# Hybrid decoder layer: memory values by seven products in half of their k groups, and the order of work at three places

## The chip, the core and the metric

The kernel runs on one core of one Trainium2 chip. The metric is the time of one execution in microseconds: median 1534.65 of three runs, 1532.35 to 1535.73. Engines: PE is TensorE, DVE is VectorE, ACT is ScalarE, POOL is GpSimd, SP is SyncE, which issues most DMAs.

## The reference

One layer in float32 with 256 positions and 256 memory tokens, width 2048. What matters here:

```python
x = x + hybrid_mixer(rms_norm(x, mix_g), w_in, ...)       # causal pooling | gated delta rule, 8 heads
mem_h = rms_norm(mem, mem_norm_g)
kv = mem_h @ w_xkv                                         # keys: columns 0..2047, values: 2048..4095
pr = softmax(q @ k.T / sqrt(512)); x = x + (pr @ v) @ w_xo # 4 heads of 512
gate = causal_dwconv(h @ w_gate, conv_w, conv_b)           # h = rms_norm(x, ffn_g), 5632 columns
x = x + (silu(gate) * (h @ w_up)) @ w_down
return rms_norm(x, final_norm_g)
```

`kv` is one of seven large products; its value half is 256 x 2048 by 2048 x 2048. The decay of the delta rule comes from two small columns per head, which are scaled by the row norm of x, so it waits for the sum of squares of x.

## The kernel before

**Products.** Each float32 product is made of three TensorE products. An operand is rounded by ACT into a high part (L101, "cast") and VectorE subtracts that from the operand for the low part (L102, "remainder"); high by high, high by low and low by high go into the same PSUM bank. Weights pass one way: SP loads a raw tile of 1 MB (three buffers, tag `raw`), ACT casts and VectorE subtracts in pieces of 128 x 1024 (four buffers each, tags `whi`, `wlo`), TensorE multiplies.

**Stages**, one after the other on TensorE: input projection (eight key heads, then queries, values and gates, then pooling groups); memory keys (16 column tiles); memory values; the mixer's output; cross attention's queries; attention; its output `xo` (16 tiles, each followed by two residual additions on VectorE, L706 and L707); gate and up; down. Side work stands in lanes: generators whose next step `pump` issues behind a given matmul.

**Values.** Four column tiles of 512 by four k groups of 512: `pvs` has two PSUM banks, one for each half of the positions, and each of the 16 loads is split in two pieces and multiplied by both halves (L680 to L695): 4 x 16 x 2 x 3 = 384 matmuls of 512 columns.

**Gate and up.** Eleven blocks `b`, each of 1024 weight columns. Two of four k groups (`JS`) go by Strassen's scheme in Winograd's form: the 2 x 2 pieces of the operands are added and subtracted so that seven products do for eight; the other two (`JP`) go plainly. A block is a list of 22 steps (`KINDS` by group); "11", "22", "s3", "s1", "s2", "21", "s4" are the seven products, "p0" to "p3" the plain pieces. A step of the first kind is six matmuls (L882 to L884), a plain one twelve. `load` issues the weight tile of a step, `prepare` makes cast and remainder four steps ahead, and GpSimd adds a second tile by an accumulating DMA (L993) where the sum of two is wanted. `combine` and `finish_block` join the six banks `b1`, `b2`, `b3`, `b5`, `b6`, `b7` into rows c11, c12, c21, c22, which are transposed (L922) in the next block. The tiles "11" lie in `ring`, whose memory was the attention output's `oT`; all other weight tiles in a pool of eight (tag `wr`). The stationary operand is `hP`, made by `stationary(f)` in the residual's lanes, and sums of it.

**Beside the first gate block** the residual x itself is transposed and written out (`rows_of_x`, lane "xr": per step four transposes, one copy on ACT into a tile of tag `sg` with two buffers, one write by SP). The last row's norm `r3` is computed there too (`last_row`).

**Start.** x is loaded, split for the first products, and squared on ACT into `xsq`; one VectorE reduction (L276) in the job `decays` makes the row sums, placed behind the latest split at that point. Then follow norm, decay columns and two small products `gps` (L311).

**Order.** A scheduler of the language orders each engine's instructions by what they wait for and by the text; `seq` ties an instruction behind the one before it on its engine, and `issue_after` behind a given one. PSUM banks and buffers of a tag are handed out in turn; who takes one waits until its former readers are done.

Of the kernel before, what the change touches and what calls it, by code (L numbers as in the profile page):

```python
# [10 lines left out]
F32 = mybir.dt.float32  # L11
# [6 lines left out]
P = 128  # L18
# [24 lines left out]
def hybrid_trunk(ctx, tc, a, out):  # L43
# [20 lines left out]
    def job(lane, gen):  # L64
        lanes.setdefault(lane, []).append(gen)
# [132 lines left out]
    with tc.tile_pool(name="dn", bufs=1, reuse_waits="tile") as dn:  # L198
# [49 lines left out]
                    first(ps0, kt, hi[:, kt % 8, :], lo[:, kt % 8, :])  # L248
        for c in range(4):
            act.activation(xsq[:, c * 4:c * 4 + 4], xraw[c // 2][:, (c % 2) * 4:(c % 2) * 4 + 4], AF.Square)  # L250
        xsum = ev("xsum")
        nc.sync.dma_start(cst, a["cst"])
        rx, rxb, rxrun = rnorm([xsum], "rx")

# [10 lines left out]
        def decays():  # L265
# [6 lines left out]
                pe.transpose(lps[:, t * 16:(t + 1) * 16], bc[:, t * P:(t + 1) * P], cv("ident")[0:16, 0:16])  # L272
            lg = dn.tile([P, 2, 16], F32, name="lg")
            act.copy(lg.rearrange("p t c -> p (t c)"), lps[:, 0:32])
            with tc.issue_after(last_split[0].ins):
                dve.tensor_reduce(xsum, xsq.rearrange("p k t -> p t k"), AX.X, ALU.add)  # L276
            next(rxrun)
            yield from rxrun
            for t in range(2):
# [387 lines left out]
        mT = mbox[0]  # L667


        KV = big("KV", [P, 2, 16, T], F32)  # L670
# [8 lines left out]
        for n in range(4):  # L679
            pvs = [psd.tile([P, 512], F32, name="pvs", tag="d") for _ in range(2)]  # L680
            for kg in range(4):
                raw = load_raw(a["w_v"][n, kg], [P, 4, 512], "wv")
                gr = wsplit(raw, 2, "wv")
                for k in range(4):
                    kt = kg * 4 + k
                    h, l = gr[k // 2][0][:, k % 2, :], gr[k // 2][1][:, k % 2, :]
                    for m_ in range(2):
                        s = slice(m_ * P, (m_ + 1) * P)
                        pe.matmul(pvs[m_], mT[:, kt, 0, s], h, start=kt == 0, stop=False)  # L689
                        pe.matmul(pvs[m_], mT[:, kt, 0, s], l, start=False, stop=False)  # L690
                        i = pe.matmul(pvs[m_], mT[:, kt, 1, s], h, start=False, stop=kt == KT - 1)  # L691
                    if kt % 2 == 1:
                        pump(i)
            for m_ in range(2):
                act.activation(Vt[:, m_, n * 512:(n + 1) * 512], pvs[m_], AF.Copy, scale=rm[:, m_:m_ + 1])  # L695
        drain("dn")
        drain("dp")
        drain("pool")
# [189 lines left out]
    acts = {}  # L888

    def rows_of_x():  # L890
        for q in range(8):
            t, n = q % 2, q // 2
            yield
            tp = pm.tile([P, 512], F32, name="xtp", tag="t", bufs=2)
            for i in range(4):
                pe.transpose(tp[:, half(i)], xres[:, 4 * n + i, half(t)], cv("ident"))
# [169 lines left out]
    drain("xr")  # L1066


    arow = big("arow", [P, head_b, 4, T], F32)
# [163 lines left out]
```

## Time and profile before

| | |
|---|---|
| median of three runs | 1534.65 us |
| profiled execution | 1533.36 us, of which its span is 1531.6 us |
| mean granted TensorE clock | 0.992 |
| busy share of the span | PE 97%, DVE 72%, ACT 56%, POOL 14% |
| DMA | 314.95 MB, mean 206 GB/s |

All times of rows are microseconds from the start of the span unless marked ns. A row of the stage table has: the stretch, its length, then busy time and count of instructions of PE, PE's weight loads, DVE, ACT and POOL, the granted TensorE clock (1.00 is 2.4 GHz, half of it 1.2), the share of the DMA engines that were busy, GB/s. A row of the timeline has start, duration, engine, line, operation, output and inputs, shape, count, and in brackets the idle time before and who ended it. Matmuls overlap in the pipeline, so their distance from start to start, not their duration, is the pace.

### The profile page before, as it was taken

What the parts mean: (1) busy time and instruction counts of PE and PEld (TensorE: products, weight loads), DVE (VectorE), ACT (ScalarE), POOL (GpSimd) and SP (SyncE); (2) the same over time, 40 slices, a digit from 0 to 9 for tenths busy, and PEclk for the clock granted to TensorE, in tenths of its full rate; (3) what the DMA queues carried; (4) which work ended last, traced back from release to release, by engine and by line L of the source; (5) the groups of instructions that cost most, each with busy time, mean ns of one, the idle gap of its engine ahead of it and who ended that gap; (6) DMA issues with size and microseconds to landing.
All of it is one profiled execution on the core that took longest, in us unless ns stands there. A gap on an engine that the chain in (4) does not pass through costs nothing.

```text
span 1531.6 us, 20542 instructions
## 1 busy us (share of the span) xinstructions
PE 1490.8 (97%) x7722; PEld 1261.1 (82%) x7722; DVE 1099.3 (72%) x1435; ACT 856.4 (56%) x1247; POOL 221.5 (14%) x237
## 2 busy tenths in 40 slices
PE   7899999999999999999988999999999999999997
PEld 4788889888888888998877888888888888888885
DVE  6978887676544676666756898898999998455445
ACT  5555656554444544555545666666666666444433
POOL 0442532441100121000320000000000000000000
PEclk9999999999999999999999999999999999999999
DMA  6445443457555555344539888888888879755651
GB/s 225 155 176 176 151 170 126 141 173 268 190 176 190 192 191 192 138 140 163 193 129 339 248 256 261 260 256 268 269 270 242 244 217 365 249 194 191 197 188 55
DMA packets 73715, 314.95 MB, mean 206 GB/s; under 512 B 12048, under 2 KB 12432, under 8 KB 57488
## 3 DMA queue, kind: packets, MB, share of 16 engines
q1 hardware_dynamic: 67136, 290.05, 54.1%
q0 software_dynamic: 6336, 23.07, 8.4%
q8 instruction: 60, 0.98, 0.2%
q10 hardware_dynamic: 144, 0.52, 0.1%
q14 instruction: 39, 0.32, 0.1%
HBM read 304.05 MB, written 9.57 MB: 205 GB/s over the span
## 4 chain that ended last, share of the span: by engine, by line
PE 82%; DVE 7%; DMA 4%; ACT 2%; POOL 2%; issue 1%; SPq 1%; POOLq 0%; ACTq 0%; DVEq 0%
PE b L882 9%; PE b L884 9%; PE b L883 9%; PE acc L1096 5%; PE acc L1095 5%; PE acc L1094 5%; PE xq L143 4%; PE xo L143 4%; PE mix L143 4%; PE kk L143 3%; PE pvs L691 2%; PE pvs L690 2%; PE pvs L689 2%; PE xq L144 2%; PE xo L144 2%; PE mix L144 2%
## 5 line engine op out<-in xcount | busy, mean ns | idle before, releaser
L960 ACT CAST wh<-wr 128x1024 fp32r<-128x1024 f32 x154 | 160.2, 1050 | 82.4 <-DVE wr L996 30.0
L961 DVE TENSOR_TENSOR wl<-wr,wh 128x1024 fp32r<-128x1024 f32 x154 | 185.2, 1219 | 27.1 <-ACT wh L960 26.0
L882 PE MATMUL b<-wh,hP 128*128 128x512 f32 x484 | 192.4, 398 | 8.0 <-ACT wh L960 5.5
L884 PE MATMUL b<-wh,hP 128*128 128x512 f32 x484 | 191.8, 397 | 0.0
L883 PE MATMUL b<-wl,hP 128*128 128x512 f32 x484 | 190.6, 394 | 1.0 <-DVE wl L961 1.0
L961 DVE TENSOR_TENSOR wl<-wd,wh 128x1024 fp32r<-128x1024 f32 x88 | 107.5, 1224 | 101.9 <-ACT wh L960 100.3
L960 ACT CAST wh<-wd 128x1024 fp32r<-128x1024 f32 x88 | 92.7, 1054 | 118.5 <-PE acc L1096 115.7
L961 DVE TENSOR_TENSOR wl<-ring,wh 128x1024 fp32r<-128x1024 f32 x88 | 106.5, 1220 | 31.9 <-ACT wh L960 31.8
L960 ACT CAST wh<-ring 128x1024 fp32r<-128x1024 f32 x88 | 91.5, 1051 | 63.5 <-PE b L884 24.8
L1094 PE MATMUL acc<-wh,aring 128*128 128x512 f32 x320 | 124.5, 389 | 0.0
L1095 PE MATMUL acc<-wl,aring 128*128 128x512 f32 x320 | 124.5, 389 | 0.0
L1096 PE MATMUL acc<-wh,aring 128*128 128x512 f32 x320 | 124.5, 389 | 0.0
L882 PEld LDWEIGHTS b<-wh,hP 128*128 128x128 f32 x484 | 91.9, 190 | 28.0 <-ACT wh L960 5.8
L102 DVE TENSOR_TENSOR wil<-wi,wih 128x1024 fp32r<-128x1024 f32 x78 | 100.3, 1293 | 16.1 <-ACT wih L101 15.8
L883 PEld LDWEIGHTS b<-wl,hP 128*128 128x128 f32 x484 | 91.9, 190 | 20.3 <-DVE wl L961 1.9
L884 PEld LDWEIGHTS b<-wh,hP 128*128 128x128 f32 x484 | 91.8, 190 | 18.8
L993 POOL DMA_DIRECT2D ring<-in_w_gu x44 | 38.5, 879 | 422.2 <-DVE sg L932 343.1
L101 ACT CAST wih<-wi 128x1024 fp32r<-128x1024 f32 x78 | 81.4, 1048 | 18.0 <-DMA wi<-in_w_in 6.3
L143 PE MATMUL xq<-h2T,wqh 128*128 128x512 f32 x240 | 84.9, 393 | 0.0
L143 PE MATMUL kk<-mT,wkh 128*128 128x512 f32 x240 | 84.4, 393 | 0.0
L143 PE MATMUL xo<-oT,woh 128*128 128x512 f32 x240 | 84.3, 392 | 0.0
L143 PE MATMUL mix<-yT,wmh 128*128 128x512 f32 x240 | 84.1, 392 | 0.0
(466 smaller groups left out, 3769.9 us busy)
## 6 DMA issues: line engine op xcount, KB each, us to landing
wr<-in_w_gu SPq DMA_DIRECT2D x156, 512.0 KB, 7.0
wd<-in_w_down SPq DMA_DIRECT2D x88, 512.0 KB, 4.8
wi<-in_w_in SPq DMA_DIRECT2D x39, 1024.0 KB, 5.0
ring<-in_w_gu POOLq DMA_DIRECT2D x44, 512.0 KB, 7.4
wk<-in_w_k SPq DMA_DIRECT2D x16, 1024.0 KB, 4.9
wv<-in_w_v SPq DMA_DIRECT2D x16, 1024.0 KB, 4.8
wm<-in_w_mix SPq DMA_DIRECT2D x16, 1024.0 KB, 4.9
wq<-in_w_xq SPq DMA_DIRECT2D x16, 1024.0 KB, 4.9
```

Of the source, the lines that this page charges most:

```text
L101: act.copy(hi, src)
L102: return dve.tensor_tensor(lo, src, hi.bitcast(F32), ALU.subtract)
L143: pe.matmul(ps, h, full, start=kk == 0, stop=False)
L144: i = pe.matmul(ps[:, T:], l, xt[:, 0, :], start=False, stop=False)
L882: pe.matmul(ps, xh, wh, start=first and i == 0, stop=False, skip_group_check=True)
L883: pe.matmul(ps, xh, wl, start=False, stop=False, skip_group_check=True)
L884: m = pe.matmul(ps, xl, wh, start=False, stop=last and i == 1, skip_group_check=True)
L960: cast[:] = [put(act.copy(h, src))]
L961: less[:] = [put(dve.tensor_tensor(l, src, h.bitcast(F32), ALU.subtract))]
L1094: pe.matmul(acc[t, n], ah, wh, start=first, stop=False)
L1095: pe.matmul(acc[t, n], ah, wl, start=False, stop=False)
L1096: return pe.matmul(acc[t, n], al, wh, start=False, stop=last)
```

## The change

Four edits. (1) The value product runs over two pairs of column tiles, `c`; of the four k groups, 0 and 1 go by seven products and 2 and 3 plainly, in 22 steps per pair, 360 matmuls in all. A job `memory_sums` makes the sums of the memory tiles during key tile 8; sums of weight tiles are VectorE additions and one accumulating DMA by GpSimd per piece. (2) The first gate block's tiles "11" take buffers of tag `wr` in place of the ring. (3) The rows of x go through one tile of four places (tag `ac`), are written by GpSimd's queue, and are stepped by the block's loop at steps 3 to 19; the norm job of the last row yields six times first. (4) The sum of squares is five additions in place of the reduction, placed before the decays.

```diff
+        for c in range(1, 4):
+            dve.tensor_tensor(xsq[:, 0:4], xsq[:, 0:4], xsq[:, 4 * c:4 * c + 4], ALU.add)
+        dve.tensor_tensor(xsq[:, 0:2], xsq[:, 0:2], xsq[:, 2:4], ALU.add)
         xsum = ev("xsum")
+        dve.tensor_tensor(xsum, xsq[:, 0], xsq[:, 1], ALU.add)
...
-            with tc.issue_after(last_split[0].ins):
-                dve.tensor_reduce(xsum, xsq.rearrange("p k t -> p t k"), AX.X, ALU.add)
...
+        def memory_sums():
+            for g in range(2):
+                tmp = dn.tile([P, 2, 4, T], F32, name="mtmp", tag="kall", bufs=1)
...
+                dve.tensor_tensor(am, mg[:, :, 0].bitcast(F32), mg[:, :, 1].bitcast(F32), ALU.add)
+                yield
...
+                dve.tensor_tensor(s5, a21, a22, ALU.subtract)
+                dve.tensor_tensor(s7, a11, a21, ALU.subtract)
+                yield
+                dve.tensor_tensor(s6, a11, s5, ALU.subtract)
+                dve.tensor_tensor(s3, a12, s6, ALU.subtract)
+                yield
+                for w in range(2):
+                    split(s[w], s[2 + w], tmp[:, 1, 2 * w:2 * w + 2])
+                yield
...
+        def values():
...
+            up = ((("b3", A11), ("b2", A21)), (("b3", A12), ("b2", A22)))
+            low = ((("b1", A11), ("b7", A21)), (("b1", A12), ("b7", A22)))
+            one = lambda *u: (u, u)
+            KINDS = (("11", one(("b1", A11))), ("u2", up), ("22", one(("b3", S3))), ("s1", one(("b5", S5))), ("u3", up),
+                     ("s3", one(("b7", S7))), ("s2", one(("b6", S6))), ("21", one(("b1", A12))),
+                     ("l2", low), ("l3", low), ("s4", one(("b7", A22))))
...
+            def prepare(c, kind, h, uses):
...
+                seq(act.copy(hi, s))
+                seq(dve.tensor_tensor(lo, s, hi.bitcast(F32), ALU.subtract))
+                ready[c, kind, h] = hi, lo
+                if kind == "22":
+                    if h == 0:
+                        T4[c] = dn.tile([P, 4, 512], F32, name="vsum", tag="kall", bufs=1)
+                    seq(dve.tensor_tensor(T4[c][:, two], raw[c, "11"][h], raw[c, "12"][h], ALU.add))
+                if kind == "u3":
+                    r = raw[c, "12"][h]
+                    seq(dve.tensor_tensor(r, r, raw[c, "22"][h], ALU.add))
+                if kind == "s3":
+                    r = T4[c][:, two]
+                    seq(dve.tensor_tensor(r, r, raw[c, "22"][h], ALU.add))
+                if kind == "s2":
+                    nc.gpsimd.dma_start(s, a["w_v"][2 * c, h][:, 2:4], accum_op=ALU.add)
...
+            AHEAD, NS, nl = 3, 22, 0
+            for s in range(-AHEAD, len(steps)):
+                while nl < len(loads) and due[loads[nl]] <= s + AHEAD + 10:
+                    fetch(*loads[nl])
+                    nl += 1
+                if s + AHEAD < len(steps):
+                    prepare(*steps[s + AHEAD])
...
+                combine(s // NS, s % NS)
+                multiply(*steps[s])
+            last_part(1)
...
+            if f == 8:
+                for lane in ("dn", "dp", "pool"):
+                    drain(lane)
+                job("ms", memory_sums())
...
     def rows_of_x():
+        rows = fp.tile([P, 4, 512], F32, name="xt", tag="ac", bufs=1)
...
-            xt = fp.tile([P, 512], F32, name="xt", tag="sg", bufs=2)
-            act.copy(xt, tp)
-            nc.sync.dma_start(xspill[t, :, n * 512:(n + 1) * 512], xt)
-            yield
+            yield
+            seq(act.copy(rows[:, q % 4], tp))
+            nc.gpsimd.dma_start(xspill[t, :, n * 512:(n + 1) * 512], rows[:, q % 4])
...
-        job("r", run)
+        def later():
+            for _ in range(6):
+                yield
+            yield from run
+
+        job("r", later())
...
-        if kind == "11":
+        if kind == "11" and b:
...
-    job("xr", rows_of_x())
+    leaving = rows_of_x()
...
+        if 3 <= s < 20:
+            next(leaving, None)
```

The functions not shown in the diff do what their namesakes of the gate stage do: `fetch` issues the loads of a kind, `multiply` its matmuls (banks b2 and b7 come from the pool `psg`, the other four from `psd`), `combine` and `last_part` join the banks by three VectorE operations at step 14, two at step 18, one at the end, with ACT scaling between them.

**VectorE at the start.** The piece of the difference after the first key tile's remainders (`w0l`); `wil` are the remainders of the next key tiles, `bc` the decay columns, `rxms` the norm.

```order
-L268 TENSOR_TENSOR bc<-bps,bc 16x256
-L102 TENSOR_TENSOR wil<-wi,wih 128x1024 x2
-L276 TENSOR_REDUCE xsum<-xsq 128x256
-L102 TENSOR_TENSOR wil<-wi,wih 128x1024
+L252 TENSOR_TENSOR xsq<-xsq 128x1024 x2
+L272 TENSOR_TENSOR bc<-bps,bc 16x256
+L252 TENSOR_TENSOR xsq<-xsq 128x1024
+L253 TENSOR_TENSOR xsq<-xsq 128x512
+L255 TENSOR_TENSOR xsum<-xsq 128x256
+L102 TENSOR_TENSOR wil<-wi,wih 128x1024 x4
 L171 TENSOR_SCALAR rxms<-rxps 128x2
```

The reduction stood between the second and the third remainder; the five additions stand before the first. The two products `gps` come 12 matmuls earlier in TensorE's order.

**VectorE in the values.** Before, the middle of the stage is remainders `wvl` alone:

```order
L102 TENSOR_TENSOR wvl_4382<-wv_4375,wvh_4381 128x1024
L102 TENSOR_TENSOR wvl_4412<-wv_4409,wvh_4411 128x1024
L102 TENSOR_TENSOR wvl_4416<-wv_4409,wvh_4415 128x1024
L102 TENSOR_TENSOR wvl_4450<-wv_4447,wvh_4449 128x1024
L102 TENSOR_TENSOR wvl_4454<-wv_4447,wvh_4453 128x1024
```

In the change, from the first "22" piece of the first pair on (`vsum` and `wv12` are the sums; wv_4337 is "11", wv_4342 "22", wv_4349 "u3"):

```order
L756 TENSOR_TENSOR wvl_4378<-wv_4342,wvh_4377 128x1024
L761 TENSOR_TENSOR vsum_4381<-wv_4337,wv12_4345 128x1024
L756 TENSOR_TENSOR wvl_4390<-wv_4342,wvh_4389 128x1024
L761 TENSOR_TENSOR vsum_4381<-wv_4337,wv12_4346 128x1024
L756 TENSOR_TENSOR wvl_4411<-vsum_4381,wvh_4410 128x1024
L756 TENSOR_TENSOR wvl_4430<-vsum_4381,wvh_4429 128x1024
L756 TENSOR_TENSOR wvl_4442<-wv_4349,wvh_4441 128x1024
L764 TENSOR_TENSOR wv12_4345<-wv12_4345,wv_4342 128x1024
L756 TENSOR_TENSOR wvl_4453<-wv_4349,wvh_4452 128x1024
L764 TENSOR_TENSOR wv12_4346<-wv12_4346,wv_4342 128x1024
L756 TENSOR_TENSOR wvl_4465<-wv12_4345,wvh_4464 128x1024
L767 TENSOR_TENSOR vsum_4381<-vsum_4381,wv_4342 128x1024
```

Six additions per pair stand between the remainders.

**SP and TensorE at the first gate product.** Rows with their waits: the engines whose counters the instruction waits for (DMAHW and DMASW are DMA queues). Before, SP:

```order
L110 DMA wo_7597<-in_w_xo 128x2048 [waits DMAHW0_49,DVE_49]
L987 DMA ring_7653<-in_w_gu 128x1024 [waits PE_49]
L987 DMA ring_7653<-in_w_gu 128x1024
L987 DMA wr_7658<-in_w_gu 128x1024 [waits DVE_49,Pool_49]
L987 DMA wr_7660<-in_w_gu 128x1024
```

In the change, SP:

```order
L110 DMA wo_7703<-in_w_xo 128x2048 [waits DMAHW0_49,DVE_49]
L1138 DMA wr_7762<-in_w_gu 128x1024 [waits DVE_49,PE_49,Pool_49]
L1138 DMA wr_7764<-in_w_gu 128x1024 [waits PE_49]
L1138 DMA wr_7766<-in_w_gu 128x1024
L1138 DMA wr_7768<-in_w_gu 128x1024
```

The first load now stands on the last `wo` remainders and on earlier work, not on the last `xo` matmul; the first `ring` load stands nine places behind it. Before, TensorE:

```order
L140 MATMUL xo_7607<-oT_5673,wol_7604 128x256
L141 MATMUL xo_7607<-oT_5673,woh_7603 128x512
L882 MATMUL b1_7709<-wh_7674,hP_6978 128x512 [waits PE_49,Activation_49]
L883 MATMUL b1_7709<-wl_7675,hP_6978 128x512 [waits DVE_49]
L884 MATMUL b1_7709<-wh_7674,hP_6978 128x512
```

In the change, TensorE:

```order
L140 MATMUL xo_7713<-oT_5779,wol_7710 128x256
L141 MATMUL xo_7713<-oT_5779,woh_7709 128x512
L1028 MATMUL b1_7817<-wh_7782,hP_7084 128x512 [waits DVE_49,PE_49,Activation_49]
L1029 MATMUL b1_7817<-wl_7783,hP_7084 128x512
L1030 MATMUL b1_7817<-wh_7782,hP_7084 128x512
```

The first product's bank `b1` has a new wait for VectorE: four banks more are taken out of three in the values, so its bank is that of the last `xo` tile, where before it was that of the tile ahead of it. VectorE's order there is the same in both: the remainder of the last rows of `hP`, two remainders of "11", the first residual addition of the last `xo` tile, a remainder, the second addition, two remainders.

## Rows read from the trace of the kernel before

**Rows 1.** Busy time by stretch; columns as told above.

```profile
900.00:1260.00 360.00, 360.00 (x1653) 296.14 (x1652) 326.91 (x357) 238.79 (x280) 29.04 (x34) 1.00 0.85 254
840.00:845.00 5.00, 5.00 (x17) 3.94 (x16) 2.52 (x3) 2.66 (x4) 0.00 (x0) 0.66 1.02 408
```

**Rows 2.** Waits: engine, tile, line, releaser: total us, times, longest.

```profile
PE b L882 <- ACT wh L960: 5.5, 1, 5.5
...
PE b L882 <- DVE ring L1019: 2.5, 1, 2.5
...
PE gps L311 <- DVE gg L304: 1.9, 1, 1.9
...
SPq L987 <- PE xo L141: 25.0, 1, 25.0
```

**Rows 3.** Timeline of TensorE, values stage: start, duration, instruction.

```profile
409.43 0.40 PE L689 MATMUL pvs<-wvh,mT 128*128 128x512 f32 x1
...
499.03 0.39 PE L143 MATMUL mix<-yT,wmh 128*128 128x512 f32 x1
```

**Rows 4.** Lines: instruction xcount, busy us, mean ns, idle before.

```profile
L102 DVE TENSOR_TENSOR wvl<-wv,wvh 128x1024 fp32r<-128x1024 f32 x32 | 39.6, 1238 | 45.4 <-ACT wvh L101 45.4
...
L101 ACT CAST wvh<-wv 128x1024 fp32r<-128x1024 f32 x32 | 33.5, 1047 | 43.6 <-PE pvs L691 40.9 <-PE kk L143 2.7
...
L996 DVE TENSOR_TENSOR wr<-wr 128x1024 f32<-128x1024 f32 x22 | 26.8, 1219 | 2.5 <-DMA wr<-in_w_gu 2.5
```

**Rows 5.** Timeline of VectorE at the start.

```profile
19.93 0.41 DVE L268 TENSOR_TENSOR bc<-bps,bc 16x256 f32<-16x256 f32 x1 [2.07 <-ACT bc L267]
23.32 2.36 DVE L102 TENSOR_TENSOR wil<-wi,wih 128x1024 fp32r<-128x1024 f32 x2 [2.98 <-ACT wih L101]
25.59 7.44 DVE L276 TENSOR_REDUCE xsum<-xsq 128x256 f32<-128x4096 f32 x1
```

**Rows 6.** DMA issues: KB each, us to landing.

```profile
wv<-in_w_v SPq DMA_DIRECT2D x16, 1024.0 KB, 4.8
```

**Rows 7.** Line L993: issue ns min/median/max, first and last start; landing.

```profile
L993 POOL DMA_DIRECT2D ring<-in_w_gu x44: 857/868/1060, 798.7 to 1259.7; - x44
...
DMA to landing us min/median/max: 5.6/7.4/12.3
```

**Rows 8.** Timeline of TensorE, first gate block.

```profile
831.83 0.39 PE L883 MATMUL b<-wl,hP 128*128 128x512 f32 x1
...
835.00 0.39 PE L882 MATMUL b<-wh,hP 128*128 128x512 f32 x1
```

**Rows 9.** Chain of waits: start, duration, instruction (transposes of L922).

```profile
859.25 0.47 PE gt L922 x3
...
947.13 0.49 PE ut L922 x4
...
989.89 0.49 PE ut L922 x4
```

**Rows 10.** Timeline around the first gate product, VectorE, then TensorE.

```profile
772.13 1.23 DVE L102 TENSOR_TENSOR hP<-hc,hP 128x1024 fp32r<-128x1024 f32 x1 [0.57 <-ACT hP L101]
...
788.56 0.96 DVE L102 TENSOR_TENSOR hP<-hc,hP 128x768 fp32r<-128x768 f32 x1 [1.81 <-ACT hP L101]
...
799.24 0.42 DVE L706 TENSOR_TENSOR xres<-xo,xres 128x256 f32<-128x256 f32 x1
...
791.00 0.39 PE L141 MATMUL xo<-oT,woh 128*128 128x512 f32 x1
```

**Rows 11.** Timeline of TensorE: last matmuls of key tiles one to four.

```profile
31.74 0.39 PE L141 MATMUL in_k<-hT,wih 128*128 128x512 f32 x1
...
40.98 0.39 PE L141 MATMUL in_k<-hT,wih 128*128 128x512 f32 x1
...
47.32 0.39 PE L141 MATMUL in_k<-hT,wih 128*128 128x512 f32 x1
...
52.88 0.39 PE L141 MATMUL in_k<-hT,wih 128*128 128x512 f32 x1
```

More of the change, by code (lines that the diff above doesn't have):

```diff
@@ new lines, in values, with seq, plain, mixed @@
+        def values():
+            latest = {}
+            def seq(i):
+                e = i.ins.engine
+                if e in latest:
+                    tc.add_manual_dep(i.ins, latest[e], NOSYNC, reason="in the order of the text")
+                latest[e] = i.ins.name
+                return i
+            hf = lambda t: slice(t * P, (t + 1) * P)
+            def plain(t, k):
+                return lambda g, i: (mT[:, 4 * g + k + i, 0, hf(t)], mT[:, 4 * g + k + i, 1, hf(t)])
+            def mixed(w):
+                return lambda g, i: (mS[g][0][w // 2][:, w % 2, hf(i)], mS[g][1][w // 2][:, w % 2, hf(i)])
+            A11, A12, A21, A22 = (plain(t, k) for t in range(2) for k in (0, 2))
+            S5, S6, S7, S3 = (mixed(w) for w in range(4))
+            up = ((("b3", A11), ("b2", A21)), (("b3", A12), ("b2", A22)))
[4 more added lines that the diff above has]
+                     ("l2", low), ("l3", low), ("s4", one(("b7", A22))))
+            ENDS = {"b5": "s1", "b6": "s2", "b3": "u3", "b2": "u3", "b1": "l3", "b7": "s4"}
+            PART = {"11": (0, 0), "12": (1, 0), "22": (1, 2), "21": (0, 2)}
+            steps = [(c, kind, half_, uses[half_]) for c in range(2) for kind, uses in KINDS for half_ in range(2)]
+            loads = [(c, kind) for c in range(2) for kind in ("11", "u2", "22", "12", "u3", "21", "l2", "l3")]
+            due = {}
+            for n, (c, kind, h, _) in enumerate(steps):
+                due.setdefault((c, {"s1": "12"}.get(kind, kind)), n)
+            raw, ready, bk, held, T4 = {}, {}, {}, {}, {}
+            def fetch(c, kind):
+                if kind[0] in "ul":
+                    r = load_raw(a["w_v"][2 * c + (kind[0] == "u"), int(kind[1])], [P, 4, 512], "wv")
+                    raw[c, kind] = [r[:, 2 * g:2 * g + 2] for g in range(2)]
+                    return
+                n, k = PART[kind]
+                if kind == "12":
+                    r = [dn.tile([P, 2, 512], F32, name="wv12", tag="u4", bufs=2) for g in range(2)]
+                else:
+                    r = st.tile([P, 4, 512], F32, name="wv", tag="raw", bufs=3)
+                    r = [r[:, 2 * g:2 * g + 2] for g in range(2)]
+                raw[c, kind] = r
+                for g in range(2):
+                    nc.sync.dma_start(r[g], a["w_v"][2 * c + n, g][:, k:k + 2])
+            def prepare(c, kind, h, uses):
+                two = slice(2 * h, 2 * h + 2)
+                if kind in ("s1", "s2", "s4"):
+                    s = T4[c][:, two]
+                else:
+                    s = raw[c, "12" if kind == "s3" else kind][h]
+                hi = st.tile([P, 2, 512], F32R, name="wvh", tag="whi", bufs=4)
+                lo = st.tile([P, 2, 512], F32R, name="wvl", tag="wlo", bufs=4)
+                seq(act.copy(hi, s))
[13 more added lines that the diff above has]
+                    nc.gpsimd.dma_start(s, a["w_v"][2 * c, h][:, 2:4], accum_op=ALU.add)
+            def multiply(c, kind, h, uses):
+                hi, lo = ready.pop((c, kind, h))
+                g = int(kind[1]) if kind[0] in "ul" else h
+                for name, stat in uses:
+                    begins = (c, name) not in bk
+                    if begins:
+                        pool_, tag = (psg, "g") if name in ("b7", "b2") else (psd, "d")
+                        bk[c, name] = pool_.tile([P, 512], F32, name="pvs", tag=tag)
+                    ends = h == 1 and ENDS[name] == kind
+                    ps = bk[c, name]
+                    for i in range(2):
+                        xh, xl = stat(g, i)
+                        seq(pe.matmul(ps, xh, hi[:, i], start=begins and i == 0, stop=False, skip_group_check=True))
+                        seq(pe.matmul(ps, xh, lo[:, i], start=False, stop=False, skip_group_check=True))
+                        seq(pe.matmul(ps, xl, hi[:, i], start=False, stop=ends and i == 1, skip_group_check=True))
+            def out(c, t, n):
+                return Vt[:, t, (2 * c + n) * 512:(2 * c + n + 1) * 512]
+            def combine(c, k):
+                o = lambda name: bk[c, name]
+                if k == 3:
+                    held["q1"], held["u2"] = (dn.tile([P, 512], F32, name=n, tag="C", bufs=2) for n in ("vq1", "vu2"))
+                    seq(act.copy(held["q1"], o("b1")))
+                q1, u2 = held.get("q1"), held.get("u2")
+                if k == 14:
+                    seq(dve.tensor_tensor(u2, o("b6"), q1, ALU.subtract))
+                    seq(dve.tensor_tensor(q1, o("b5"), u2, ALU.add))
+                    seq(dve.tensor_tensor(out(c, 1, 1), q1, o("b7"), ALU.subtract))
+                if k == 16:
+                    for t_, s in ((out(c, 1, 1), 1), (q1, 0), (u2, 1)):
+                        seq(act.activation(t_, t_, AF.Copy, scale=rm[:, s:s + 1]))
+                if k == 18:
+                    for t, name, s in ((0, "b3", q1), (1, "b2", out(c, 1, 1))):
+                        seq(dve.scalar_tensor_tensor(out(c, t, 1), o(name), rm[:, t:t + 1], s, ALU.mult, ALU.add))
+                if k == 21:
+                    seq(act.activation(out(c, 0, 0), o("b1"), AF.Copy, scale=rm[:, 0:1]))
+            def last_part(c):
+                seq(dve.scalar_tensor_tensor(out(c, 1, 0), bk[c, "b7"], rm[:, 1:2], held["u2"], ALU.mult, ALU.subtract))
+            AHEAD, NS, nl = 3, 22, 0
[5 more added lines that the diff above has]
+                    prepare(*steps[s + AHEAD])
+                if s < 0:
+                    continue
+                if s == NS + 1:
+                    last_part(0)
+                combine(s // NS, s % NS)
+                multiply(*steps[s])
+            last_part(1)
@@ L676, in hybrid_trunk @@
                 drain("mem")
+            if f == 8:
+                for lane in ("dn", "dp", "pool"):
+                    drain(lane)
+                job("ms", memory_sums())
             m = evac(ps, "k")
             pool.tensor_tensor(Kt[:, f, :], m, rmb, ALU.mult)
[L679 to L695, printed above, removed]
+        drain("ms")
+        values()
         drain("dn")
@@ L895, in rows_of_x @@
             for i in range(4):
[L896 to L899 removed]
+                seq(pe.transpose(tp[:, half(i)], xres[:, 4 * n + i, half(t)], cv("ident")))
             yield
+            seq(act.copy(rows[:, q % 4], tp))
+            nc.gpsimd.dma_start(xspill[t, :, n * 512:(n + 1) * 512], rows[:, q % 4])
     latest = {}
@@ L1065, in hybrid_trunk @@
     job("cv", finish_block(NB - 1))
-    drain("xr")
     arow = big("arow", [P, head_b, 4, T], F32)
```

8 lines of the change are left out of this document (added).

## The prediction

> **What bounds the kernel now.** I read the stage table first, then TensorE's waits, then the order of time around the three edited places. In the table the reader is to see that through most of the run TensorE has no idle time at all: in the 360 us from 900 to 1260 it is busy 360.00 us at full clock, while VectorE has 326.91 us of work [rows 1]. There only fewer matmuls help. The list of waits shows the exceptions, which lie in the first 80 us and around 791 to 840: 5.5 us for the first gate product's cast, 2.5 us for a combination of the first gate block, 1.9 us for the decay sums [rows 2]. The change works at one place of the first kind (the memory values) and two of the second.
>
> **Memory values.** The stage runs from 409.43 to 499.03, 89.60 us for 384 matmuls, evenly 0.2333 us apart [rows 3], so TensorE bounds it. The change has 360: of four k groups two go by seven products instead of eight. 24 x 0.2333 = 5.6 us go, if TensorE stays fed.
>
> Feeding it: each half of 22 steps takes 180 x 0.2333 = 42.0 us, a step of six matmuls 1.4, of twelve 2.8. ACT casts 22 pieces of 1.05 us, VectorE subtracts 22, adds 6 of the same size and combines; a subtraction of 1024 columns takes 1.24 and two in a row 2.36, an addition of that size 1.22 [rows 4, 5]. That is about 28 x 1.2 + 4 = 38 of 42 us on VectorE, so lateness must be followed in its order. I set the stage's start to 0. A piece is cast when the piece four before it has been multiplied. Piece 4 ("22", first half) is cast at 1.4, its remainder done at 3.7 and the first sum at 4.9; pieces 5, 6, 7 follow at 6.1, 8.5, 10.7. The "u3" tile's load waits for the second "u2" remainder (2.7) and lands 4.8 later [rows 6] at 7.5, before its slot is free at 9.8; remainders at 12.1 and 14.5 against steps 8 and 9 at 14.0 and 16.8. Then the pairs of remainder and addition: "s3" done at 16.9 and 19.3 (needed 19.6, 21.0), "s2" at 21.7 and 22.9 (needed 22.4, 23.8). This is the tightest place, 0.7 to 0.9 us. Pieces to "l2" end at 27.7, and the three combinations behind them (an estimate of 0.7 each from the 1024-column row) at 29.7. Bank b7 may take its next product only then; TensorE is there at 28.0 + 1.4 = 29.4. I book 0.3 per half. The accumulating DMAs leave at 21.7 and 22.9 and land 7.4 later, at worst 12.3 [rows 7]: 29 to 35, read at step 20 (39.2), with the casts some microseconds before it. The net is -5.6 + 0.6 = -5.0.
>
> Bounds: the gate blocks' matmuls stand 3.17 / 14 = 0.2264 apart [rows 8]; at that pace the stage takes 81.5, a gain of 8.1. From the other side, the first gate block shows what this scheme costs when it is not fed (rivals). I take the stage's own pace, since tiles, buffers and stationary are the same.
>
> The sums of the memory tiles (two groups of one 1024-column addition, four of 512 columns, two casts, two remainders: some 12 us of VectorE) lie in the key stage, whose matmuls run without a gap up to 409.43, and are done seven key tiles ahead; with that cover gone they would cost those 12 us.
>
> **First gate block.** Its first tiles go into the ring, which takes the attention output's place; SP waits 25.0 us for the last output matmul, and all loads behind stand still [rows 2]. That matmul starts at 791.00 and ends at 791.39 [rows 10]. The mark of the next block, its transposes at step 26, comes at 859.25 [rows 9]. Unhindered, 26 steps are 216 matmuls at 0.2264 = 48.9, and the 32 row transposes (a block of 989.89 - 947.13 = 42.76 us [rows 9] less 180 x 0.2264 = 40.75 leaves 0.126 for each of its 16) 4.0. So the block loses 859.25 - 791.39 - 52.9 = 15.0 us: the waits of [rows 2], half clock, and casts that queue on ACT behind row copies.
>
> In the change the loads wait for the split at 772.13 (done at 773.4 [rows 10]) instead, and have 15 us before ACT, done with the last rows of hP when the remainder starts at 788.56, is free for them. Row copies have four places in place of two, their DMAs leave SP, and one transpose group follows every second step. What is late next is not a load: banks are handed out in turn, and four more allocations out of three banks let the first product fall on the bank of the last output tile. So its first matmul now waits for that tile's second residual addition, and VectorE has splits in front of it. The hP remainder ends at 788.56 + 0.96 = 789.5, two remainders (casts done at 789.6 and 790.6) at 792.0, first addition 0.42 [rows 10], a third remainder 793.6, second addition 794.0. TensorE stands from 791.39 to 794.0, 2.6 us, where it stood 5.5. After the wait of 2.5 before 839.1 the granted clock was 0.66 over the next 5 us [rows 1], partly at 1.2 GHz: 1.7 us lost. I book the same. The mark then falls at 791.39 + 2.6 + 1.7 + 52.9 = 848.6: -10.7.
>
> I followed the later steps from 794: "22" and "p1" are in place, the third kind's second tile is loaded after 789.5, summed by 801 and wanted at about 808; two of eight load slots now hold the gate tiles for twenty steps, but "p2", the tile loaded latest, lands near 808 and is wanted at 814. Bounds: no wait and no slow clock give the whole 15.0; if the later waits all stay, only 5.5 - 2.6 = 2.9 goes; a loss is possible only by the two slots, and I take it as at most 0 to 2.
>
> A page speaks against moving the row DMAs to GpSimd. Its own DMA issues took 857 to 1060 ns, 44 times [rows 7], beside a VectorE that is 91% busy [rows 1]. The Trainium skill ("SBUF — State Buffer", section "SBUF: two separate sides") says that VectorE, with certain operations on two SBUF inputs or in its faster modes, locks GpSimd out of a shared port, and that GpSimd then cannot write descriptors; it tells of a transfer that went from 620 to 3100 ns. By that factor, 12 issues in the first block would be 4.3 us each instead of 0.87, 52 us of GpSimd in a block of 43, and its accumulations would come late; the trace does not bear it out, so the sum takes 0.87.
>
> **Start.** One reduction of 7.44 us stands on VectorE from 25.59 to 33.03, in front of the second key tile's remainder, though VectorE was idle before 19.93 and for 2.98 us before 23.32 [rows 5]. The additions (3 x 1.22, and half and a quarter of that: about 4.6 us) come before 23.3 by the order and fit into that idle time. The second key tile took 40.98 - 31.74 = 9.24 us, the fourth, unhindered, 52.88 - 47.32 = 5.56 [rows 11]. Difference -3.7, which contains the two waits and the half clock after them. Behind it the decay chain (1.9 us of wait [rows 2]) starts about as much earlier, but its matmuls also stand 12 places (2 us) earlier on TensorE; I leave that wait as it is. Bounds: the chain keeps its old time and eats everything (0), or its wait goes as well (-5.6).
>
> **Sum.** -3.7 - 5.0 - 10.7 = -19.4 against the profiled run's 1533.36 us (span 1531.6): 1514.0. The median of the runs is 1.3 us above that run, so 1515.2; I say 1515.
>
> **Rivals.**
> 1. Loads starve the values. Place: the three raw buffers of 1 MB, which sums hold long ("11" until 7, "22" until 20). For it: in the first gate block the same scheme lost 15.0 us. Against: the stage's loads land in 4.8 us, and "u3" stands 6 us of slack. Price: 2 x 15.0; 1533.4 - 3.7 - 10.7 - 5.6 + 30 = 1543.4, median 1545, slower. It decides from a loss of 0.45 us per step on; every load would have to land some 9 us after its issue.
> 2. The first gate block stays starved behind its first step: only 2.9 there, 1523. For it: two slots fewer, and DMA busy through the block. Against: loads begin 18 us earlier and SP is no longer held by row writes.
> 3. The decay chain takes the start's gain back: 1519. For it: the earlier places on TensorE.
> 4. The reserve: values at 0.2264, or no wait for the bank: 1508 to 1512.
>
> **Chances.** Forecast with its nearer spread (1512 to 1518) 0.5; rival 4, 0.12; rival 3, 0.15; rival 2, alone or with a slower feed of the values, 0.17; rival 1, 0.06, of which some still lands near zero. The forecast's own range is 1511 to 1519; with rivals 2 to 4 the range is 1508 to 1526. About 3 us (0.2%) is what a measurement can tell: faster 0.93, same 0.03, slower 0.04.
>
> **What would show it.** Values: 84 to 85 us between the first value matmul and the first mix matmul, with no wait over 0.5 us in it; longer gaps at "s2" or "u3" mean rival 1. First gate block: a wait of 2 to 3 us for VectorE's second residual addition, half clock for some 3 us, then no wait; waits of matmuls for casts or loads mean rival 2. Start: second key tile in under 6 us, no reduction, decay sums waiting 1 to 3 us; 4 or more means rival 3. The forecast is wrong if the sum of the three differences misses the total by more than 3 us, that is, if another stage moved.

## The result, and the profile after

The median is 1518.2 us (four runs, 1517.6 to 1521.0) for 1534.7: ratio 0.9898, 95% interval 0.9881 to 0.9915. The forecast was 1515 with 1508 to 1526. The profiled execution took 1517.59 us, its span 1515.8, so 15.8 us less of span than before, where 19.4 had been booked. Measured on TensorE from mark to mark (from start to start of the matmuls named):

| stretch on TensorE | before | after | difference | booked |
|---|---|---|---|---|
| start to the last matmul of the input projection | 314.06 | 311.06 | -3.0 | -3.7 |
| from there to the last key matmul | 95.13 | 99.25 | +4.1 | 0 |
| values | 89.60 | 84.92 | -4.7 | -5.0 |
| mixer output to the last `xo` matmul | 291.97 | 291.97 | 0 | 0 |
| last `xo` matmul to the first gate transposition | 66.81 | 53.41 | -13.4 | -10.7 |
| from there to the first down matmul | 422.15 | 422.10 | 0 | 0 |
| down, first to last matmul | 241.03 | 242.23 | +1.2 | 0 |

The total came out near the forecast because misses of opposite sign met: the keys' stage lost 4.1 us that nobody had booked, down another 1.2 and the start 0.7, and the first gate block gave 2.7 more than its term. That is luck, not the forecast's merit. The marks of the first two rows, before and then after:

```profile
314.06 0.39 PE L141 MATMUL in_u<-hT,wih 128*128 128x512 f32 x1
...
409.19 0.40 PE L141 MATMUL kk<-mT,wkh 128*128 128x512 f32 x1
```

```profile
311.06 0.40 PE L141 MATMUL in_u<-hT,wih 128*128 128x512 f32 x1
...
410.31 0.40 PE L141 MATMUL kk<-mT,wkh 128*128 128x512 f32 x1
```

**Start.** VectorE, as in [rows 5]: the first two of the five additions, the last, and the next remainders.

```profile
16.42 2.54 DVE L252 TENSOR_TENSOR xsq<-xsq 128x1024 f32<-128x1024 f32 x2
...
21.17 0.42 DVE L255 TENSOR_TENSOR xsum<-xsq 128x256 f32<-128x256 f32 x1
22.02 1.23 DVE L102 TENSOR_TENSOR wil<-wi,wih 128x1024 fp32r<-128x1024 f32 x1 [0.42 <-ACT wih L101]
```

The additions lie ahead of 22.02 and cover the time in which VectorE was idle. The last matmuls of key tiles one to four, as in [rows 11]:

```profile
30.94 0.39 PE L141 MATMUL in_k<-hT,wih 128*128 128x512 f32 x1
...
36.50 0.39 PE L141 MATMUL in_k<-hT,wih 128*128 128x512 f32 x1
...
42.82 0.39 PE L141 MATMUL in_k<-hT,wih 128*128 128x512 f32 x1
...
52.31 0.63 PE L141 MATMUL in_k<-hT,wih 128*128 128x512 f32 x1
```

The second tile now takes 36.50 - 30.94 = 5.56 us for 9.24, but the fourth 52.31 - 42.82 = 9.49 for 5.56. The list of waits shows why; this row answers to the third one of [rows 2], which had 1.9:

```profile
PE gps L313 <- DVE gg L306: 3.0, 1, 3.0
```

`gps` starts at 50.25 for 55.79, in the fourth tile now and not in the fifth. About 1 us more of the fourth tile's loss came with a lower clock: behind the new wait the granted clock was 0.68, partly at 1.2 GHz, and behind the wait of 1.9 before the change it was 1.00. After and before, columns as in [rows 1]:

```profile
50.00:55.00 5.00, 4.75 (x20) 4.20 (x21) 4.60 (x13) 2.56 (x5) 1.23 (x2) 0.68 0.50 175
```

```profile
55.00:60.00 5.00, 4.21 (x25) 3.79 (x26) 4.70 (x13) 1.87 (x3) 2.34 (x2) 1.00 0.55 205
```

**Keys.** VectorE and then TensorE, near the end of the last head pair's delta rule:

```profile
338.10 1.21 DVE L682 TENSOR_TENSOR mtmp<-mT 128x1024 f32<-128x1024 f32 x1
...
339.70 0.41 DVE L686 TENSOR_TENSOR mtmp<-mtmp 128x256 f32<-128x256 f32 x1
...
342.71 0.16 DVE L552 TENSOR_TENSOR f<-f,sq__3149 128x4 f32<-128x4 f32 x1 [0.91 <-POOL f L551]
...
343.13 0.87 DVE L554 TENSOR_SCALAR o<-o,f 128x128 f32<-128x128 f32 x4
...
343.46 0.92 PE L560 MATMUL otp<-cst,o 128*128 128x128 f32 x4 [2.37 <-DVE o L554]
```

`mtmp` (L682, L686) are memory sums. They stand in VectorE's order around the short steps `f` and `o` of the delta rule, and TensorE waits 2.37 us for `o`. TensorE's waits between 305 and 372 us, before and then after:

```profile
PE w L529 <- DVE R L522: 0.4, 1, 0.4
```

```profile
PE otp L560 <- DVE o L554: 2.4, 1, 2.4
PE w L531 <- DVE R L524: 1.1, 1, 1.1
```

The text places the sums at memory key tile 8, but nothing held them there on VectorE, and the first of them ran at 317.8, while the matmuls of that tile begin at 366.1. (The key tiles here are the 16 of the memory; the loss lies in the first five.)

**Values.** First matmul, the one that follows the first half's bank, and the first one of the next stage, as in [rows 3]:

```profile
410.56 0.40 PE L783 MATMUL pvs<-wvh,mT 128*128 128x512 f32 x1
...
440.32 0.50 PE L783 MATMUL pvs<-wvh,mT 128*128 128x512 f32 x1 [0.25 <-DVE KV L799]
...
495.48 0.39 PE L143 MATMUL mix<-yT,wmh 128*128 128x512 f32 x1
```

360 matmuls in 84.92 us, with one gap in each half: the matmul that takes b7 starts 29.76 us behind the stage's start.

**First gate block.** VectorE, TensorE, and the first transpositions; the group of three answers to the 859.25 of [rows 9]:

```profile
785.01 0.96 DVE L102 TENSOR_TENSOR hP<-hc,hP 128x768 fp32r<-128x768 f32 x1 [1.81 <-ACT hP L101]
...
788.24 0.42 DVE L852 TENSOR_TENSOR xres<-xo,xres 128x256 f32<-128x256 f32 x1
...
789.71 0.42 DVE L853 TENSOR_TENSOR xres<-xo,xres 128x256 f32<-128x256 f32 x1
...
787.45 0.39 PE L141 MATMUL xo<-oT,woh 128*128 128x512 f32 x1
790.27 0.47 PE L1028 MATMUL b<-wh,hP 128*128 128x512 f32 x1 [2.44 <-DVE xres L853]
...
840.86 0.27 PE L1068 MATMUL gt<-cst,ring 128*128 128x128 f32 x1
...
842.21 0.55 PE L1068 MATMUL gt<-cst,ring 128*128 128x128 f32 x3
```

The table and the experiments count to the first single transposition, 840.86 here and 857.81 before; [rows 9] and the prediction count to the group of three behind it:

```profile
857.81 0.27 PE L922 MATMUL gt<-cst,ring 128*128 128x128 f32 x1
```

The first product waits 2.44 us for the second residual addition, in place of the 5.5 us of [rows 2]; TensorE's list of waits has no other one up to the mark. The stage table says what the clock did (columns as in [rows 1]):

```profile
900.00:1260.00 360.00, 360.00 (x1652) 296.63 (x1651) 326.79 (x359) 239.94 (x282) 28.46 (x33) 1.00 0.86 258
788.00:793.00 5.00, 2.73 (x12) 2.29 (x13) 4.24 (x6) 3.55 (x6) 2.39 (x3) 1.00 0.84 165
793.00:798.00 5.00, 5.00 (x26) 4.15 (x25) 5.00 (x6) 2.23 (x3) 0.00 (x0) 1.00 1.01 291
```

The clock stayed at 2.4 GHz behind the wait, and VectorE's 326.79 us of 360 in the blocks after are those of [rows 1]. GpSimd's issues in the first block, accumulations and writes of rows (duration in ns, min, median, max):

```profile
L1144 POOL DMA_DIRECT2D wr<-in_w_gu x4: 857/895/914, 787.5 to 812.9; - x4
```

```profile
L1046 POOL DMA_DIRECT2D xspill<-xt x8: 539/566/897, 801.3 to 832.2; - x8
```

### The profile page after: what moved, and what is told of

Read it like the earlier page. It is cut to its first block, busy times and chain, and to the rows that moved or that the text cites. A ratio compares the mean times of both kernels' runs of the same rounds, so it can differ in the third digit from the quotient of the medians.

```text
span 1515.8 us, 20595 instructions
## 1 busy us (share of the span) xinstructions
PE 1479.2 (98%) x7698; PEld 1253.6 (83%) x7698; DVE 1137.3 (75%) x1489; ACT 870.9 (57%) x1265; POOL 230.6 (15%) x249
## 4 chain that ended last, share of the span: by engine, by line
PE 81%; DVE 8%; ACT 4%; POOL 3%; DMA 3%; issue 2%; SPq 0%; POOLq 0%; DVEq 0%; ACTq 0%
PE b L1028 10%; PE b L1030 10%; PE b L1029 10%; PE acc L1246 5%; PE acc L1247 5%; PE acc L1248 5%; PE xq L143 4%; PE mix L143 4%; PE xo L143 3%; PE kk L143 3%; PE xq L144 2%; PE mix L144 2%; PE xo L144 2%; PE pvs L783 2%; PE pvs L785 2%
## 5 line engine op out<-in xcount | busy, mean ns | idle before, releaser
L1111 ACT CAST wh<-wr 128x1024 fp32r<-128x1024 f32 x162 | 168.4, 1050 | 87.5 <-DVE wr L1147 30.2
L1112 DVE TENSOR_TENSOR wl<-wr,wh 128x1024 fp32r<-128x1024 f32 x162 | 194.7, 1218 | 26.3 <-ACT wh L1111 25.1
L1111 ACT CAST wh<-ring 128x1024 fp32r<-128x1024 f32 x80 | 83.2, 1051 | 53.6 <-PE b L1030 29.4
L1112 DVE TENSOR_TENSOR wl<-ring,wh 128x1024 fp32r<-128x1024 f32 x80 | 96.7, 1218 | 21.4 <-ACT wh L1111 21.4
L102 DVE TENSOR_TENSOR wil<-wi,wih 128x1024 fp32r<-128x1024 f32 x78 | 99.9, 1287 | 15.8 <-ACT wih L101 15.4
L1144 POOL DMA_DIRECT2D ring<-in_w_gu x40 | 34.6, 865 | 379.4 <-DVE sg L1078 365.2
L143 PE MATMUL xq<-h2T,wqh 128*128 128x512 f32 x240 | 84.9, 393 | 0.0
L143 PE MATMUL mix<-yT,wmh 128*128 128x512 f32 x240 | 84.1, 392 | 0.0
```

Of the source, the lines that this page charges most:

```text
L143: pe.matmul(ps, h, full, start=kk == 0, stop=False)
L1111: cast[:] = [put(act.copy(h, src))]
L1112: less[:] = [put(dve.tensor_tensor(l, src, h.bitcast(F32), ALU.subtract))]
```

## The experiments

Each kernel was timed beside the kernel before on the same chip; ratios are against it, with 95% intervals. Four chips were used, and the kernel before had medians of 1533.5 to 1534.0 us on them and 1534.7 in the first measurement, so a difference of about 1 us between kernels of different chips can't be read. Each kernel has one trace.

**One part alone.** Three kernels, each the kernel before with one part of the diff: `start` with the additions, `values` with `memory_sums` and `values`, `gate` with the tiles, the rows and the later norm.

```diff
# start
-                dve.tensor_reduce(xsum, xsq.rearrange("p k t -> p t k"), AX.X, ALU.add)
+        dve.tensor_tensor(xsum, xsq[:, 0], xsq[:, 1], ALU.add)
...
# values
+        drain("ms")
+        values()
...
# gate
-        if kind == "11":
+        if kind == "11" and b:
-    job("xr", rows_of_x())
+    leaving = rows_of_x()
```

> The kernel before with the additions in place of the reduction and nothing else. Theory (the 4.2 us that the changed kernel lost in its first five key tiles of the memory belong to the memory sums): nothing is lost there, the start's 3.0 us stay to the end, about 1531.7 us. Rival (they belong to the stream that reaches the last delta pair 3 us earlier, at another place of the side work): the first five key tiles lose 3 to 4 us here too, about 1535 us.

Measured: 1532.0 us, 0.9988 (0.9974 to 1.0001). The keys' stage took 94.9 us: nothing lost there. The second key tile ended 4.0 us earlier than before, the fourth 0.15 later, the input projection 1.4 earlier.

> The kernel before with the values by seven products and the memory sums, nothing else. Theory: the values' stage takes 84.9 us for 89.6 (-4.7), the first five key tiles take 4.2 us more, sum -0.5, about 1534.2 us. Rival (the loss came from the start's shift): -4.7, about 1530 us.

Measured: 1533.1 us, 0.9999 (0.9984 to 1.0014). The values took 84.93 us and the keys 99.3 for 95.1. The theory holds for these two stages: the sums come with the loss, without the start's shift. The trace is of one of the two fastest of ten executions (1528.4 to 1535.9). In it the first gate block, whose text is as before, took 63.47 us for 66.81, with one wait in place of several:

```profile
PE b L1026 <- DVE xres L851: 9.8, 1, 9.8
```

The four more banks put the first product behind the last residual addition, which stood on VectorE behind remainders of tiles that the ring let in late; the later waits of the block were gone.

> The kernel before with the two edits of the first gate block only: without the values' four extra banks the first gate product takes the bank of the last but one output tile. Theory (the 2.4 us wait is the bank's): no wait at the first product, first row transposition of the block 51.0 us behind the last output matmul for 53.4 in the changed kernel and 66.8 before: -15.8, about 1518.9 us. Rival (VectorE's queue holds the first product up whatever bank it has): the wait stays at 2 us or more, -13.4, about 1521.3 us.

Measured: 1519.8 us, 0.9916 (0.9895 to 0.9937). The first product starts 0.23 us behind the start of the last output matmul, without a wait: the wait was the bank's. But the first transposition comes after 53.94 us, not 51.0. TensorE's waits between 780 and 860 us in this kernel:

```profile
PE xtp L897 <- ACT xt L899: 1.5, 1, 1.5
```

It ran into a row transposition that waits for the copy of the row before, which stands behind casts on ACT, and the granted clock was 0.61 from 804 to 808. Removing the first wait moved it. Against the kernel before on their chip the three parts alone took off 1.4, 0.4 and 13.7 us, together 15.5, and the whole change 16.4 in its own measurement: nearly all of it is the first gate block, and the values' 4.7 us were mostly eaten by the memory sums.

**The memory sums later.**

```diff
-        dve.tensor_tensor(o, ps[:, :T], c, ALU.add)
+        last_evac[0] = dve.tensor_tensor(o, ps[:, :T], c, ALU.add)
...
-                dve.tensor_tensor(am, mg[:, :, 0].bitcast(F32), mg[:, :, 1].bitcast(F32), ALU.add)
+                with tc.issue_after(last_evac[0].ins):
+                    dve.tensor_tensor(am, mg[:, :, 0].bitcast(F32), mg[:, :, 1].bitcast(F32), ALU.add)
```

> The changed kernel with the memory sums on VectorE queued behind the reading out of key tile 8. Theory: the first five key tiles take as long as before (their loss of 4.2 us goes), the sums' 12 us of VectorE lie beside later key tiles that have no delta chain beside them, about 1514 us. Rival: the loss is only moved, because those tiles or the first value pieces are late by as much: about 1518 us.

Measured: 1514.0 us (four runs, 1512.4 to 1515.4), 0.9877 (0.9856 to 0.9898). Last matmul of the input projection and last of the keys:

```profile
311.70 0.40 PE L142 MATMUL in_u<-hT,wih 128*128 128x512 f32 x1
...
406.43 0.40 PE L142 MATMUL kk<-mT,wkh 128*128 128x512 f32 x1
```

94.73 us, as without any sums, and the values still take 84.92. With the sums early the stretch took 99.25 to 99.36 in three kernels; without them or with them late 94.4 to 95.8 in eleven. All four times lie below the four of the change (1517.6 to 1521.0); the intervals of the two ratios overlap (0.9881 to 0.9915 for the change), so the stage's 4.5 us are shown by the traces and the total's gain is likely, not certain.

**The bank.**

```diff
-                        pool_, tag = (psg, "g") if name in ("b7", "b2") else (psd, "d")
+                        pool_, tag = (psg, "g") if name in ("b7", "b2") or (c, name) == (1, "b5") else (psd, "d")
```

> The changed kernel with one of the values' banks taken from the other pool, so that the first gate product no longer takes the bank of the last output tile. Theory, after the run with the gate's two edits alone (no wait at the first product, yet the first transposition of the block came 53.9 us behind the last output matmul, and 53.4 with the wait): TensorE only runs into the next late thing, the copy of the rows that stands behind casts on ACT, so the 2.4 us come back as another wait and half clock; 53 to 54 us, total as the changed kernel, 1518. Rival, the prediction's: the wait is a loss by itself, 51.0 us, total 1515.8.

Measured: 1517.2 us, 0.9899 (0.9883 to 0.9916); the first transposition after 52.36 us for 53.41. Between the two: of the 2.4 us, 1.5 came back as the same wait for the row copy as in `gate`, this time at full clock. The total can't be told from the change's.

```profile
PE xtp L1043 <- ACT xt L1045: 1.5, 1, 1.5
```

**The halves of the gate edit.** `tiles`: only the tiles 11 out of the ring. `rows`: only the rows and the later norm.

> The kernel before with the first gate block's tiles 11 out of the ring and the rows of x left as they were. From the last output matmul to the first transposition of the block it took 66.8 us before and 53.9 with both edits. Theory: the first wait of 5.5 us and the half clock behind it go, the waits for row copies and for the combination stay: 58 to 60 us, total 1526. Rival: TensorE starts at once and meets the row copies earlier, most comes back: over 63 us, total 1531.

Measured: 1531.3 us, 0.9985 (0.9975 to 0.9994); 64.88 us from the last output matmul to the transposition, for 66.81. The rival holds. TensorE's waits there:

```profile
PE xtp L896 <- ACT xt L898: 3.6, 3, 1.6
PE b L882 <- DVE ring L1019: 2.4, 1, 2.4
PE b L882 <- ACT wh L960: 2.1, 1, 2.1
PE b L883 <- DVE wl L961: 1.4, 2, 0.8
PE r3ps L166 <- POOL sq L716: 1.3, 1, 1.3
```

> The kernel before with the rows of x through four places, by GpSimd's queue and stepped by the loop, and the tiles 11 left in the ring. Theory: the 5.5 us stay with their half clock (some 9 us over the unhindered 52.9), the later waits (1.7, 1.0, 2.5 us and a second half clock) go: 60 to 62 us, total 1528. Rival: the later waits come from loads that start late behind the ring, not from the rows: over 64 us, total 1532.

Measured: 1529.9 us, 0.9973 (0.9963 to 0.9984); 62.23 us. Waits:

```profile
PE b L882 <- ACT wh L965: 5.4, 1, 5.4
PE xtp L897 <- ACT xt L899: 2.5, 1, 2.5
PE b L883 <- DVE wl L966: 0.5, 1, 0.5
```

The halves give 1.9 and 4.6 us, both together 12.9 (`gate`): each alone leaves the other's waits in the way, and a stretch of half clock with them (0.81 and 0.77 from 836 to 844 in `tiles`, 0.65 and 0.50 from 792 to 800 in `rows`).

**The addresses.** In the kernel with late sums, a pad of 32 bytes moves the split tiles, and whatever else lies behind it.

```diff
         xsum = ev("xsum")
+        st.tile([P, 8], F32, name="pad", tag="pad", bufs=1)
```

> The changed kernel with the late memory sums (1514.0), and a pad of 32 bytes that moves the split tiles of the weights to addresses that are multiples of 64, as those of the gate stage are. Value matmuls stand 0.2333 us apart, gate matmuls 0.2264. Theory: the address of the moving operand makes the difference; the values' stage goes from 84.9 to about 82.4, total 1511.5. Rival: it is something else in the stage (what else is read and written beside it); 84.9 stays, total 1514.

Measured: 1520.9 us, 0.9920 (0.9905 to 0.9934), 6.8 us slower than without the pad. The values took 84.12 us, a third of what the theory said; but every plain tile, where the same split tiles are the stationary operand, became slower. Two tiles' last matmuls of the mixer's output, with the pad and without:

```profile
516.81 0.39 PE L142 MATMUL mix<-yT,wmh 128*128 128x512 f32 x1
...
522.46 0.39 PE L142 MATMUL mix<-yT,wmh 128*128 128x512 f32 x1
```

```profile
513.58 0.39 PE L142 MATMUL mix<-yT,wmh 128*128 128x512 f32 x1
...
519.14 0.40 PE L142 MATMUL mix<-yT,wmh 128*128 128x512 f32 x1
```

5.65 us a tile for 5.56, and so in nearly every plain tile, from the second key tile of the input projection on. The pad did change the pace, so addresses matter to it, but the rule that was tried is not it; which tile's address counts, and how, is open.

**The decay chain.** Late sums, and `gps` two yields later:

```diff
-            for _ in range(7):
+            for _ in range(9):
```

> The changed kernel with the late memory sums (1514.0) and the decay chain's two small products about three microseconds later in TensorE's order. Theory (the start's gain of 3.5 to 4.5 us at the second key tile is taken back at the fourth, because the earlier products wait 3.0 us for the decay chain and half clock follows): fourth key tile as long as before the change, the wait below 0.5 us, total about 1511. Rival: what hangs behind the chain (decay matrices, key pairs) is late by as much and the wait only changes its name: about 1514.

Measured: 1518.4 us, 0.9903 (0.9880 to 0.9927), 4.3 us slower than with late sums alone. The fourth key tile took 5.56 us, as the theory said, and at the end of the first query tile the kernel was 5.8 us ahead of the one with late sums alone; but then an inverse's product waits:

```profile
PE qp L426 <- DVE Z L421: 4.8, 2, 4.6
...
PE gps L314 <- DVE gg L307: 1.5, 1, 1.5
```

4.6 of the 4.8 us are one wait, at 152, where there were 1.5 us in all; from 152 to 162 the granted clock was 0.75 and then 0.57. The rival holds: the wait took another name.

**The queue of the rows.** Late sums, with the rows written by SP again:

```diff
-            nc.gpsimd.dma_start(xspill[t, :, n * 512:(n + 1) * 512], rows[:, q % 4])
+            nc.sync.dma_start(xspill[t, :, n * 512:(n + 1) * 512], rows[:, q % 4])
```

> The changed kernel with the late memory sums (1514.0) and the eight writes of the rows of x on SP's queue again; the four places and the steps stay. Theory: with four places nothing waits for a write soon, but SP's queue stands at each write until its copy on ACT is done, and the gate tiles' loads behind it are late: first transposition of the block 1 to 3 us later than 53.4, total 1516. Rival: the places and the steps are what counts and the queue is not: 53.4 us, total 1514.

Measured: 1514.8 us, 0.9872 (0.9844 to 0.9901); 53.38 us. In this kernel the queue makes no difference: the four places, the steps and the later norm, which were not taken apart, do the work.

**Late sums with the old start**, then **with the bank**. The edits are the first diff above taken back, and the bank's diff.

> The changed kernel with the late memory sums (1514.0), and the start as it was before (the one reduction in place of five additions). Theory (the decay chain takes most of the start's gain back): the start is worth 0 to 2 us at the end, total 1514 to 1516. Rival (the prediction's term): 3.7 us, total 1517.7.

Measured: 1517.1 us, 0.9893 (0.9875 to 0.9911), between the two. In the profiled executions the input projection ended 1.3 us later than with the additions, and 1.6 more came from half clock behind the 2.4 us wait at the gate, which this execution had and the other not (the mark at 54.99 and 53.40). `start` alone gave 1.4 us with an interval that reaches to nothing, here it is 3.0 between two chips: what the start is worth stays open between 0 and 3 us.

> The changed kernel with both mends that took time off: the memory sums behind key tile 8 and one of the values' banks from the other pool. Theory (they lie in different stages and add up: -4.2 and -1.0 against 1518.2): 1513. Rival: the second mend's 1.0 was the spread between two runs: 1514.

Measured: 1513.7 us (six runs, 1512.7 to 1520.8), 0.9871 (0.9851 to 0.9890). Not to be told from 1514.0; the mark came at 53.34 in its trace, no earlier than without the bank. The one execution at 1520.8 was the profiled one; it has a wait of 3.2 us at the first transpositions (842.65), with half clock behind it, that no other trace shows, and its cause is open.

## Why the prediction was right, and where its steps were not

**The total: in the range by luck.** The prediction's own last sign speaks against it: the sum of the three differences is -3.0 - 4.7 - 13.4 = -21.1 us for a total of -15.8, a miss of 5.3 where 3 was to be the limit, because another stage moved, the keys.

**Values: right in mechanism and in size.** -4.7 for -5.0. The pace stayed at 0.233, and the place where it was to be late was the one: the b7 combination was booked to end at 29.7 us, and the matmul that waits for it started at 29.76. It cost 0.5 us a half, not 0.3. No matmul waited for a load, so rival 1 fell.

**Memory sums: the step that failed.** That the sums "lie in the key stage, whose matmuls run without a gap up to 409.43" was read from the values' end of that stage. In its first five tiles the last head pair's chain still runs on VectorE in short steps for which TensorE waits, and there the 12 us of sums were not covered: +4.1, and in the run with the sums alone 99.3 for 95.1. With the sums held behind key tile 8 on VectorE (`sums_late`) the stretch took 94.73 again. The term was booked at nothing; where VectorE's queue really puts the sums, and what they cost between those steps, was not asked.

**First gate block: mechanism right, size low by 2.7.** The bank's wait came as described, 2.44 for 2.6, by the same instructions in the same order. Two terms were off. Half clock was booked at 1.7; this execution had none, nor had `sums_late` and `late_rows_sp`, while three others with the same wait (`late_no_start`, `late_chain`, `late_align`) had it, with marks at 54.9 to 55.0 for 53.4. These kernels have nearly the same text there, so the term comes and goes, and what decides it is open. And the unhindered block was 1 us too long: mark at 842.21 - 787.84 = 54.4, less the wait 51.9 for 52.9. That the wait was a loss of its own was also mostly wrong: without it `gate` has its mark no earlier, and `bank` 1.0 us earlier. Nothing of rival 2 was seen: the block has no later wait. The slow issues that the prediction weighed from the Trainium skill ("SBUF — State Buffer", section "SBUF: two separate sides") did not come: GpSimd's issues took 857 to 914 ns and 539 to 897, within the range of [rows 7] or shorter, and with late sums the time was the same with the rows on SP (1514.8 and 1514.0). The page tells of the missing descriptors for VectorE's two-port mode, and of the lock by two SBUF inputs only against a GpSimd operation that reads SBUF; the prediction left these conditions out, and no run here shows whether the block meets them.

**Start: the gain came, and was mostly taken back.** -4.5 at the second key tile, -0.6 at the fourth, -1.1 at the seventh: rival 3, as far as there. The chain's products stand earlier on TensorE and wait 3.0 us for 1.9, and half clock followed (0.68 from 50 to 55), where none did before; the prediction had left this wait as it is. Its sign for rival 3, a wait of 4 us or more, did not show, so the sign was set too high. The -3.0 of the table at 311 us holds more than the edit: kernels with the same start differ by up to 4 us there (311.8 to 315.9 with the old one in six executions, 311.1 to 313.8 with the new in six, means 313.4 and 312.2; `late_chain` and `late_align`, which change this stage, are left out).

**Down: not the change.** The stage took 241.0 to 242.6 us over kernels that do the same there.

## What to carry to other kernels

Work that is moved under cover must be followed to the place where the queue really puts it: an edge on the engine that does it, not on another, holds it there, and "the engine is idle on average" says nothing beside a chain of short steps. Where two waits stand one behind the other, removing one is worth little (1.9 and 4.6 us here, in one trace each) and removing both much (12.9), so price them together, and ask for each wait that goes what TensorE meets next and how late that is. A stage measured from mark to mark in several traces shows what a sum over the whole run hides when two misses cancel.

## What was not expected of the hardware

A pad of 32 bytes ahead of the split tiles changed TensorE's pace evenly: plain tiles 5.65 us for 5.56 (+1.6%), values 84.1 for 84.9. And the wait of 2.4 us at the first gate product was followed by a granted clock of 0.66 to 0.68 over one stretch of 5 us in three traces, and of 1.00 throughout in three others, though the kernels have nearly the same text there.
